# SSM phase tables built behind the first tables of the products, and an output stage in two equal parts of 516 tokens

## The chip, the cores and the metric

The kernel runs on one core of one Trainium2 chip. The metric is the device time of the whole program in microseconds (us), the median of several runs. PE is TensorE, DVE VectorE, ACT ScalarE, POOL GpSimd, SP the engine on which the DMAs are issued.

## The reference

One inference step of one decoder layer, for a prompt of 2048 tokens and 8 sample tokens of one position each, with D = 1024:

```python
h = rmsnorm(x, g_pre)
c_a, c_b, c_z, s_x, s_z, g_c, g_s = split(h @ w_in)   # 3 x 1024, 2 x 512, 2 x 1024 columns
u = c_a * sigmoid(c_b)
v = causal_depthwise_conv(u, 31 taps) + conv_b
y_c = (silu(layernorm(v)) * silu(c_z)) @ w_pc
ys = gelu(ssm(s_x))                    # 32 groups of 16 channels, 64 complex states each
ys = ys * sigmoid(ys @ w_glu + b_glu) * silu(s_z)
m = sigmoid(g_c) * y_c + sigmoid(g_s) * (ys @ w_ps)
x = x + rmsnorm(m @ w_out, g_post)
x = x + rmsnorm(p @ w_ple, g_ple) * sigmoid(x @ w_pg + b_pg)
```

The SSM is a diagonal complex recurrence. Its parameters are discretised first: exponentials, sine and cosine of `a * exp(log_dt)`, and from these the powers of each pole and its phase at 128 steps. Besides `y`, the last 30 inputs of the convolution and the last SSM states are returned.

## The kernel before

**Halves and products.** The tokens are taken in two halves: h=0 has 1024 prompt tokens and the 8 sample tokens, 1032 columns in three blocks of 344; h=1 has 1024, in two blocks of 512 (`BLOCKS`, line 213). Every large product is made in three passes, high x high, high x low, low x high (lines 288 to 290), accumulated in a PSUM bank. A weight tile of 128 x 1024 is loaded by DMA, its high part cast by ACT (`whi`, line 251), its low part subtracted on POOL (`wlo`, line 331 by way of `w_split`). `order` (lines 217 to 233) fixes the succession of weight tiles, which is that of the products: `w_ple`, the SSM's input SX, pairs CB and CA of the convolution's input, GC, SZ, `w_glu`, two GS tiles with a `w_ps` tile four times, CZ, `w_pc`, then `w_out` and `w_pg`, each as often as the output stage has parts.

**The planner.** All instructions are put out while the program is built, in an order that a planner finds (`Background`, lines 28 to 105). Products are the foreground. Everything else is written as generators that yield the engine they want next and the time at which their inputs are ready. The planner keeps a PE clock and one clock each for DVE (V), ACT (S) and POOL (G); `use(engine, cost)` books a step on its clock, with costs that are written into the code. After each block of products, `pump` puts out every background step whose start is not later than the PE clock, the smallest priority number first. Each engine then executes its instructions in that order. `cV(n)` is 0.08 + n/960, the booked cost of a DVE operation on n columns. `Units` is a pool of 38 buffers; `room(k)` waits in the plan until k are free.

**The SSM's tables.** `ssm_setup` (line 449) discretises the parameters, then builds the phase tables: a prelude (pole magnitudes `rho`, eight-step phases), and for each half x of the channels 7 doubling steps of `ph` (lines 566 to 588), stored by DMA in `ph_d`. After that it makes, for each batch b = 0 to 3 of 8 groups, the tables of the SSM's products: `gt` on DVE (line 601), transposed on PE (line 609), small products (line 619), `kd`, and on POOL `cq` (lines 646 to 651); each is stored by DMA. `ssm_batch` (line 675) loads them (`we`, `phu`), runs the products of a batch on PE (line 719), turns the result by the phases, scans, turns it back and runs the output products (lines 774 and 777).

**The convolution.** `conv_task` (line 820) has priority 10: for each of 8 channel tiles one operation at line 844 and taps at line 851, each an operation of DVE on 1024 columns, booked at 1.33. Where 8 or more units are free when a tile starts (line 839), `conv_side` (line 867) takes taps from the far end on ACT (lines 872 and 881) and POOL, and DVE adds the two sums; this is called the POOL partner below. The DVE operations between taps are evacuations of products: `u` (CA times the sigmoid of CB) and `gs` (`w_ps` times GS).

**Layer norm and `w_pc`.** `ln_task` (line 1262) follows the last convolution tile: sum, mean by a product, differences, squares, norm, and per tile the SiLU, the product with `cz`, and the split in `vh` and `vl`. `bg.drain(ln)` (line 1321) stands ahead of the `w_pc` products.

**The output stage** (lines 1378 to 1486). `parts` are runs of blocks. For every part all 8 tiles of `w_out` are run; `o_task` sums squares; `x1_task` and its tiles `x1_tile` (line 1395) norm, scale, add x and split into `mh` and `ml`. Then for every part the 8 tiles of `w_pg` are run over `x1`, and `y_task` (line 1442) makes `y`. `next_h_task` prepares h of the second half meanwhile. In the first half part 0 is one block of 344, part 1 two blocks of 344.

Of the kernel before, what the change touches and what calls it, by code (L numbers as in the profile page):

```python
# [27 lines left out]
class Background:  # L28
# [66 lines left out]
    def use(self, e, cost, ready=0.0):  # L95

        if e == "P":
            self.pe += cost
            self.now = max(self.now, self.pe)
            return self.pe + 0.25  # L100
        self.clock[e] = max(self.clock[e], ready) + cost
        return self.clock[e] + 0.2
# [31 lines left out]
def build(nc, tc, A, O):  # L134
# [23 lines left out]
    with ExitStack() as ctx:  # L158
# [17 lines left out]
        def tt(out, a, b, op=ALU.mult):  # L176
            V.tensor_tensor(out=out, in0=a, in1=b, op=op)  # L177

        def ts(out, a, s1, s2=None, op0=ALU.mult, op1=ALU.add):
            V.tensor_scalar(out=out, in0=a, scalar1=s1, scalar2=s2, op0=op0, **({} if s2 is None else {"op1": op1}))  # L180
# [32 lines left out]
        BLOCKS = [[(0, 344), (344, 344), (688, 344)], [(0, 512), (512, 512)]]  # L213
        PARTS = [[[0], [1, 2]], [[0], [1]]]
        TOK = [HT + NS, HT]

# [229 lines left out]

        tables = {"done": 0}

        def ssm_setup():
# [19 lines left out]
            exp_dve(mag, th, (k1, k2), ki)  # L469
            r0 = use("V", 5.6, 3.0)  # L470
            yield "V", r0
# [6 lines left out]
            ts(th, th, -3.1415925, 3.1415925, ALU.max, ALU.min)  # L478
            r0 = use("V", 1.6, r0)
            yield "S", r0  # L480
# [23 lines left out]
            tt(fim, k1, k3)  # L504
            r0 = use("V", 4.0, r0)
            yield "V", r0
# [17 lines left out]
            cmul(b3(bb, 0), b3(bb, 1), fb[0], fb[1], b3(bcu, 0), b3(bcu, 1), b3(bb, 2), b3(bb, 3))  # L524
            r0 = use("V", 6.0, r0)
            use("G", 1.5, r0)
# [13 lines left out]
            for b in range(NB):  # L540
                dma(out=tt_d[b], in_=zero.rearrange("p (q x) -> p q x", q=1).to_broadcast([P, 8, P]))

            yield "V", r0
            tt(k1, mag, mag)
            tt(k1, k1, k1)
            tt(rho, k1, k1)
            ph = [[k1, k2], [k3, nre]]

            def unit_length(re, im, t):

                tt(t[0], re, re)
                tt(t[1], im, im)
                tt(t[0], t[0], t[1], ALU.add)
                ts(t[0], t[0], -0.5, 1.5)
                tt(re, re, t[0])
                tt(im, im, t[0])

            v2 = [wk[:, x * 16:x * 16 + 16] for x in range(2)]
            V.tensor_copy(out=ph[0][0], in_=cs)
            V.tensor_copy(out=ph[0][1], in_=sn)  # L560
            for x in range(3):
                unit_length(*ph[0], v2)
                cmul(*ph[1], *ph[0], *ph[0], *v2)
                ph.reverse()
            r0 = use("V", 6.5, r0)
            for x in range(2):
                yield from room(3)
                pu2 = [alloc(name="ph") for _ in range(3)]
                un = [t[:, 0:1024].rearrange("p (j k) -> p j k", k=P) for t in pu2[0:2]]
                w2 = [pu2[2][:, y * 512:(y + 1) * 512].rearrange("p (j k) -> p j k", j=8) for y in range(2)]  # L570
                s2 = [t[:, 0:8] for t in v2]
                yield "V", r0
                for r in range(2):
                    V.tensor_copy(out=un[r][:, :, 0], in_=ph[0][r][:, x * 8:x * 8 + 8])
                m = 1
                while m < P:
                    unit_length(un[0][:, :, m - 1], un[1][:, :, m - 1], s2)
                    base = [u_[:, :, m - 1:m].to_broadcast([P, 8, m]) for u_ in un]
                    cmul(un[0][:, :, m:2 * m], un[1][:, :, m:2 * m], un[0][:, :, 0:m], un[1][:, :, 0:m],
                         *base, w2[0][:, :, 0:m], w2[1][:, :, 0:m])  # L580
                    m *= 2
                    r0 = use("V", 2.0 + 6 * cV(4 * m), r0)
                    yield "V", r0
                for b in range(2 * x, 2 * x + 2):
                    for r in range(2):
                        dma(out=ph_d[b][:, r * 512:(r + 1) * 512],
                            in_=pu2[r][:, (b - 2 * x) * 512:(b - 2 * x + 1) * 512], after=r0)
                free(*pu2)
            r1 = max(r0, r1)
            for b in range(NB):  # L590
# [65 lines left out]
                tables["done"] = b + 1  # L656
                tables[b] = queue["data"] + 1.0
            free(bb, bcu, cbd, pu)

# [15 lines left out]
        def ssm_batch(h, b, sx, ysb, n, ready):  # L675
# [24 lines left out]
            r = max(r, dma(out=we[:, 0:1024], in_=we_d[b], after=tables[b]))  # L700
            phu = alloc(name="sph")
            rp = dma(out=phu[:, 0:1024], in_=ph_d[b], after=tables[b])
            sc = alloc(name="sc")
# [24 lines left out]
            free(we)  # L728
            r = max(r1, rp)
            tmp, tm2 = alloc(name="stmp"), alloc(name="stmq")  # L730
# [348 lines left out]
        def half(h, hT, finish):  # L1079
# [300 lines left out]
            x1T = mT  # L1380
            parts = [[blocks[i] for i in p] for p in PARTS[h]]
            x1t = []
# [203 lines left out]
```

## Time and profile before

| what | value |
|---|---|
| time before, median of 3 runs | 1974.46 us (1973.43 to 1976.75) |
| the profiled execution's own time | 1971.99 us |
| its span in the profile | 1970.2 us |
| PE busy, share of the span | 97% |
| DVE busy, share of the span | 73% |
| granted PE clock over the span | 0.989 |

The profile shows one execution. PE is the engine that does the products, PEld its weight loads. A wait is the idle time of an engine before an instruction, put down to what ended it. The granted clock is a share of full speed: 1.00 is 2.4 GHz, 0.50 is 1.2 GHz. "L288" is line 288 of the kernel before.

### The profile page before, as it was taken

What the parts mean: (1) busy time and instruction counts of PE and PEld (TensorE: products, weight loads), DVE (VectorE), ACT (ScalarE), POOL (GpSimd) and SP (SyncE); (2) the same over time, 40 slices, a digit from 0 to 9 for tenths busy, and PEclk for the clock granted to TensorE, in tenths of its full rate; (3) what the DMA queues carried; (4) which work ended last, traced back from release to release, by engine and by line L of the source; (5) the groups of instructions that cost most, each with busy time, mean ns of one, the idle gap of its engine ahead of it and who ended that gap; (6) DMA issues with size and microseconds to landing.
All of it is one profiled execution on the core that took longest, in us unless ns stands there. A gap on an engine that the chain in (4) does not pass through costs nothing.

```text
span 1970.2 us, 26641 instructions
## 1 busy us (share of the span) xinstructions
PE 1918.5 (97%) x10386; PEld 1723.0 (87%) x10386; DVE 1442.1 (73%) x1696; ACT 765.6 (39%) x1276; POOL 784.8 (40%) x573
## 2 busy tenths in 40 slices
PE   8897999999999999999899999999999999999998
PEld 7797999999999999999798788888888888888877
DVE  6889997899899876444884479888589843442686
ACT  7424211227311364254532223444731353223542
POOL 1437623315422223253533222687743222224554
PEclk9998999999999999999899999999999999999999
DMA  8461344542122215342554463212212211422455
GB/s 315 155 203 62 100 133 141 177 144 78 51 83 78 102 50 193 116 142 93 190 197 164 172 200 123 74 60 91 71 48 75 97 67 43 160 107 77 148 189 174
DMA packets 103286, 243.58 MB, mean 124 GB/s; under 512 B 11752, under 2 KB 44648, under 8 KB 103144
## 3 DMA queue, kind: packets, MB, share of 16 engines
q1 hardware_dynamic: 102840, 241.68, 36.2%
q8 instruction: 81, 1.33, 0.3%
q14 instruction: 45, 0.37, 0.1%
q10 hardware_dynamic: 320, 0.20, 0.0%
HBM read 188.17 MB, written 54.62 MB: 123 GB/s over the span
## 4 chain that ended last, share of the span: by engine, by line
PE 85%; issue 4%; DVE 4%; POOL 2%; ACT 1%; DMA 1%; POOLq 0%; ACTq 0%; SPq 0%; DVEq 0%
PE bank L288 27%; PE bank L290 26%; PE bank L289 26%; PE bank L774 2%; POOL wlo L331 1%; PE bank L777 1%; PE bank L719 1%; DMA raw<-in_w 1%; POOL ca L331 1%; DVE sgp L331 1%; DVE o L183 0%; DVE o L331 0%; DVE ml L331 0%; DVE spar L183 0%; PE bank L308 0%
## 5 line engine op out<-in xcount | busy, mean ns | idle before, releaser
L331 POOL TENSOR_TENSOR wlo<-raw,whi 128x512 fp32r<-128x512 f32 x386 | 566.5, 1486 | 1082.2 <-ACT whi L251 1064.5
L288 PE MATMUL bank<-hh,whi 128*128 128x344 f32 (+1 forms) x1888 | 665.9, 353 | 0.9 <-ACT whi L251 0.9
L289 PE MATMUL bank<-hl,whi 128*128 128x344 f32 (+1 forms) x1888 | 659.9, 350 | 6.8 <-DVE hl L331 6.8
L290 PE MATMUL bank<-hh,wlo 128*128 128x344 f32 (+1 forms) x1888 | 661.2, 350 | 1.4 <-POOL wlo L331 1.4
L183 DVE SCALAR_TENSOR_TENSOR acc<-u,prm,acc 128x1024 f32<-128x1024 f32 x412 | 530.5, 1288 | 11.2
L289 PEld LDWEIGHTS bank<-hl,whi 128*128 128x128 f32 x1888 | 356.9, 189 | 39.4 <-DVE hl L331 7.1
L288 PEld LDWEIGHTS bank<-hh,whi 128*128 128x128 f32 x1888 | 356.4, 189 | 36.9 <-ACT whi L251 1.5
L290 PEld LDWEIGHTS bank<-hh,wlo 128*128 128x128 f32 x1888 | 356.8, 189 | 35.6 <-POOL wlo L331 2.4
L251 ACT CAST whi<-raw 128x512 fp32r<-128x512 f32 x388 | 223.9, 619 | 148.5 <-PE bank L289 68.6
L288 PE MATMUL bank<-mh,whi 128*128 128x344 f32 (+1 forms) x640 | 227.4, 355 | 7.7 <-ACT whi L251 5.8
L290 PE MATMUL bank<-mh,wlo 128*128 128x344 f32 (+1 forms) x640 | 227.1, 355 | 5.2 <-POOL wlo L331 5.1
L289 PE MATMUL bank<-ml,whi 128*128 128x344 f32 (+1 forms) x640 | 226.6, 354 | 0.3 <-DVE ml L331 0.3
L331 POOL TENSOR_TENSOR ca<-ca,cq 128x512 f32<-128x512 f32 x104 | 132.2, 1300 | 39.5 <-ACT cq L881 36.1
L288 PEld LDWEIGHTS bank<-mh,whi 128*128 128x128 f32 x640 | 122.6, 192 | 20.8 <-ACT whi L251 7.1
L290 PEld LDWEIGHTS bank<-mh,wlo 128*128 128x128 f32 x640 | 122.7, 192 | 18.9 <-POOL wlo L331 7.8
L289 PEld LDWEIGHTS bank<-ml,whi 128*128 128x128 f32 x640 | 122.5, 191 | 12.3 <-DVE ml L331 1.1
L289 PE MATMUL bank<-vl,whi 128*128 128x344 f32 (+1 forms) x320 | 111.9, 350 | 0.7 <-DVE vl L331 0.7
L288 PE MATMUL bank<-vh,whi 128*128 128x344 f32 (+1 forms) x320 | 112.2, 351 | 0.0
L290 PE MATMUL bank<-vh,wlo 128*128 128x344 f32 (+1 forms) x320 | 112.0, 350 | 0.0
L881 ACT ACTIVATE cq<-u,prm 128x512 f32<-128x512 f32 x104 | 73.4, 722 | 55.0 <-POOL ca L331 45.9
L331 DVE TENSOR_TENSOR oacc<-oacc,sq 128x344 f32<-128x344 f32 (+1 forms) x35 | 30.6, 874 | 79.2 <-ACT sq L1388 78.7
L177 DVE TENSOR_TENSOR gcl<-bank,gcl 128x344 f32<-128x344 f32 (+1 forms) x40 | 23.5, 587 | 65.7 <-PE bank L290 65.7
(213 smaller groups left out, 2447.7 us busy)
## 6 DMA issues: line engine op xcount, KB each, us to landing
raw<-in_w SPq DMA_DIRECT2D x194, 512.0 KB
cq<-cq SPq DMA_DIRECT2D x12, 512.0 KB
e<-e SPq DMA_DIRECT2D x8, 516.0 KB
rt<-e SPq DMA_DIRECT2D x8, 516.0 KB
gc<-gc SPq DMA_DIRECT2D x8, 516.0 KB
m<-gs SPq DMA_DIRECT2D x8, 516.0 KB
gcl<-gc SPq DMA_DIRECT2D x8, 516.0 KB
m2l<-m SPq DMA_DIRECT2D x8, 516.0 KB
```

Of the source, the lines that this page charges most:

```text
L177: V.tensor_tensor(out=out, in0=a, in1=b, op=op)
L183: V.scalar_tensor_tensor(out=out, in0=a, scalar=s, in1=b, op0=op0, op1=op1)
L251: S.copy(out=hi, in_=t[:, c])
L288: T.matmul(o, hi[:, w], rh[:, c0:c0 + n], start=kt == 0, stop=False)
L289: T.matmul(o, hi[:, w], rl[:, c0:c0 + n], start=False, stop=False)
L290: T.matmul(o, lo[:, w], rh[:, c0:c0 + n], start=False, stop=kt == k - 1)
L331: (V if e == "V" else GP).tensor_tensor(out=out, in0=a, in1=b, op=op)
L719: T.matmul(pvs[rr][half_[i], jj], we[:, g * P + rr * 64:g * P + rr * 64 + 64], U[:, g, 8:8 + ne], start=True, stop=True)
L774: T.matmul(pvs[i][:, jj], TW[:, :, 2 * j + i], U[:, 2 * j + i, o0:136], start=True, stop=False)
L777: T.matmul(pvs[i][:, jj], cq[half_[i], x * 512 + j * P:x * 512 + (j + 1) * P], X[half_[i], x, j, o0:136], start=False, stop=x == 1)
L881: S.activation(out=q[:, h], in_=u[:, k + x * 512:k + x * 512 + 512], func=AF.Identity, scale=w(k))
```

## The change

The prelude and the phase tables move. `phases(x)` becomes a function; the prelude and `phases(0)` stand behind the tables of b=0, `phases(1)` behind those of b=2. `ssm_batch` loads its phase tile after its first products instead of before them, and waits in the plan for `tables["phases"]`. The costs booked for the setup's and the phases' DVE work are raised. And the output stage of the first half gets its own blocks: two parts of 516 tokens, each of two blocks of 258, where it had parts of 344 and 688 in blocks of 344. The second half's stay as they were.

```diff
--- before.py
+++ after.py
@@ -212,6 +212,7 @@
         P_OF = {k: 8 // v for k, v in KT_OF.items()}
         BLOCKS = [[(0, 344), (344, 344), (688, 344)], [(0, 512), (512, 512)]]
         PARTS = [[[0], [1, 2]], [[0], [1]]]
+        OUT_PARTS = [[[(0, 258), (258, 258)], [(516, 258), (774, 258)]], [[(0, 512)], [(512, 512)]]]
         TOK = [HT + NS, HT]
 
         order = []
@@ -444,7 +445,7 @@
             ts(ki, k, 127.0, 8388608.0, ALU.add, ALU.mult)
             tt(out, q, ki.bitcast(F32))
 
-        tables = {"done": 0}
+        tables = {"done": 0, "phases": 0}
 
         def ssm_setup():
             yield from room(4)
@@ -467,7 +468,7 @@
             exp_dve(dt, k3, (k1, k2), ki)
             tt(th, are, dt)
             exp_dve(mag, th, (k1, k2), ki)
-            r0 = use("V", 5.6, 3.0)
+            r0 = use("V", 11.0, 3.0)
             yield "V", r0
             tt(th, aim, dt)
             ts(k1, th, 0.15915494309189535, MAGIC)
@@ -476,7 +477,7 @@
             stt(th, k1, -1.9350051879882812e-3, th, ALU.mult, ALU.add)
             stt(th, k1, -3.0199157663446332e-7, th, ALU.mult, ALU.add)
             ts(th, th, -3.1415925, 3.1415925, ALU.max, ALU.min)
-            r0 = use("V", 1.6, r0)
+            r0 = use("V", 2.5, r0)
             yield "S", r0
             S.activation(out=sn, in_=th, func=AF.Sin)
             S.activation(out=k1, in_=th, func=AF.Sin, scale=0.5)
@@ -502,7 +503,7 @@
             tt(k2, nre, aim)
             tt(k1, k1, k2, ALU.subtract)
             tt(fim, k1, k3)
-            r0 = use("V", 4.0, r0)
+            r0 = use("V", 7.0, r0)
             yield "V", r0
 
             def powers(t, top):
@@ -522,7 +523,7 @@
                     GP.tensor_copy(out=pwrev[r][:, p, :], in_=pw[r][:, 7 - p, :])
             fb = [f.rearrange("p (j x) -> p j x", x=1).to_broadcast([P, NJ, 16]) for f in (fre, fim)]
             cmul(b3(bb, 0), b3(bb, 1), fb[0], fb[1], b3(bcu, 0), b3(bcu, 1), b3(bb, 2), b3(bb, 3))
-            r0 = use("V", 6.0, r0)
+            r0 = use("V", 8.0, r0)
             use("G", 1.5, r0)
             GP.memset(zero, 0.0)
             yield from room(2)
@@ -539,31 +540,7 @@
             yield None, r1
             for b in range(NB):
                 dma(out=tt_d[b], in_=zero.rearrange("p (q x) -> p q x", q=1).to_broadcast([P, 8, P]))
-
-            yield "V", r0
-            tt(k1, mag, mag)
-            tt(k1, k1, k1)
-            tt(rho, k1, k1)
-            ph = [[k1, k2], [k3, nre]]
-
-            def unit_length(re, im, t):
-
-                tt(t[0], re, re)
-                tt(t[1], im, im)
-                tt(t[0], t[0], t[1], ALU.add)
-                ts(t[0], t[0], -0.5, 1.5)
-                tt(re, re, t[0])
-                tt(im, im, t[0])
-
-            v2 = [wk[:, x * 16:x * 16 + 16] for x in range(2)]
-            V.tensor_copy(out=ph[0][0], in_=cs)
-            V.tensor_copy(out=ph[0][1], in_=sn)
-            for x in range(3):
-                unit_length(*ph[0], v2)
-                cmul(*ph[1], *ph[0], *ph[0], *v2)
-                ph.reverse()
-            r0 = use("V", 6.5, r0)
-            for x in range(2):
+            def phases(x, r0):
                 yield from room(3)
                 pu2 = [alloc(name="ph") for _ in range(3)]
                 un = [t[:, 0:1024].rearrange("p (j k) -> p j k", k=P) for t in pu2[0:2]]
@@ -579,13 +556,17 @@
                     cmul(un[0][:, :, m:2 * m], un[1][:, :, m:2 * m], un[0][:, :, 0:m], un[1][:, :, 0:m],
                          *base, w2[0][:, :, 0:m], w2[1][:, :, 0:m])
                     m *= 2
-                    r0 = use("V", 2.0 + 6 * cV(4 * m), r0)
+                    r0 = use("V", 4.0 + 6 * m / 120.0, r0)
                     yield "V", r0
                 for b in range(2 * x, 2 * x + 2):
                     for r in range(2):
                         dma(out=ph_d[b][:, r * 512:(r + 1) * 512],
                             in_=pu2[r][:, (b - 2 * x) * 512:(b - 2 * x + 1) * 512], after=r0)
                 free(*pu2)
+                tables["phases"] = 2 * x + 2
+                tables["ph", x] = queue["data"] + 1.0
+                return r0
+
             r1 = max(r0, r1)
             for b in range(NB):
                 js = slice(b * 4, b * 4 + 4)
@@ -655,6 +636,33 @@
                 free(cq, wt)
                 tables["done"] = b + 1
                 tables[b] = queue["data"] + 1.0
+                if b == 0:
+
+                    yield "V", r0
+                    tt(k1, mag, mag)
+                    tt(k1, k1, k1)
+                    tt(rho, k1, k1)
+                    ph = [[k1, k2], [k3, nre]]
+
+                    def unit_length(re, im, t):
+
+                        tt(t[0], re, re)
+                        tt(t[1], im, im)
+                        tt(t[0], t[0], t[1], ALU.add)
+                        ts(t[0], t[0], -0.5, 1.5)
+                        tt(re, re, t[0])
+                        tt(im, im, t[0])
+
+                    v2 = [wk[:, x * 16:x * 16 + 16] for x in range(2)]
+                    V.tensor_copy(out=ph[0][0], in_=cs)
+                    V.tensor_copy(out=ph[0][1], in_=sn)
+                    for x in range(3):
+                        unit_length(*ph[0], v2)
+                        cmul(*ph[1], *ph[0], *ph[0], *v2)
+                        ph.reverse()
+                    r0 = use("V", 13.0, r0)
+                if b % 2 == 0:
+                    r0 = yield from phases(b // 2, r0)
             free(bb, bcu, cbd, pu)
 
 
@@ -698,8 +706,6 @@
             yield from room(4)
             we = alloc(name="swe")
             r = max(r, dma(out=we[:, 0:1024], in_=we_d[b], after=tables[b]))
-            phu = alloc(name="sph")
-            rp = dma(out=phu[:, 0:1024], in_=ph_d[b], after=tables[b])
             sc = alloc(name="sc")
             X = sc[:, 0:1096].rearrange("p (r j s) -> p r j s", r=2, j=4)
             yield "V", 0.0
@@ -726,7 +732,11 @@
                         S.copy(out=smp[:, rr, b * 4 + j0:b * 4 + j0 + 2, :], in_=pvs[rr][:, :, 128:136])
                     r1 = use("S", 0.56 if first else 0.36, r1)
             free(we)
-            r = max(r1, rp)
+            while tables["phases"] < b + 1:
+                yield None, bg.now + 1.0
+            yield from room(3)
+            phu = alloc(name="sph")
+            r = max(r1, dma(out=phu[:, 0:1024], in_=ph_d[b], after=tables["ph", b // 2]))
             tmp, tm2 = alloc(name="stmp"), alloc(name="stmq")
             E = X[:, :, :, 9:137]
             t1 = tmp[:, 0:1024].rearrange("p (r j s) -> p r j s", r=2, j=4)
@@ -1378,7 +1388,7 @@
             oT = [unit("o") for _ in range(NT)]
             acc = unit("oacc")
             x1T = mT
-            parts = [[blocks[i] for i in p] for p in PARTS[h]]
+            parts = OUT_PARTS[h]
             x1t = []
 
             def o_task(c, c0, m, r, sq):
```

## Rows read from the trace of the kernel before

**Rows 1.** The page's head and its table of engines: busy us, share, instructions.
```profile
span 1970.2 us, 26641 instructions
PE 1918.5 (97%) x10386; PEld 1723.0 (87%) x10386; DVE 1442.1 (73%) x1696; ACT 765.6 (39%) x1276; POOL 784.8 (40%) x573
```

**Rows 2.** Waits of PE over the span: us in total, times, longest.
```profile
PE bank L609 <- issue: 14.1, 1, 14.1
PE bank L288 <- ACT whi L251: 13.1, 6, 6.3
```

**Rows 3.** Windows: us, busy PE, PEld, DVE, ACT, POOL (instructions), PEclk, DMA, GB/s.
```profile
192.00:196.00 4.00, 0.00 (x0) 0.00 (x0) 3.82 (x9) 0.00 (x0) 0.00 (x0) 0.50 0.67 231
196.00:200.00 4.00, 3.83 (x15) 3.86 (x16) 3.93 (x7) 1.21 (x2) 1.28 (x1) 0.50 0.40 135
200.00:204.00 4.00, 4.00 (x23) 3.98 (x22) 3.93 (x5) 0.79 (x2) 0.00 (x0) 0.77 0.00 0
```

**Rows 4.** Windows of the first half's output stage, end of `w_out` and start of `w_pg`.
```profile
938.50:956.00 17.50, 17.35 (x108) 16.65 (x107) 10.06 (x8) 12.65 (x20) 11.70 (x8) 1.00 0.60 211
956.00:990.00 34.00, 23.32 (x103) 20.64 (x103) 33.03 (x34) 12.50 (x21) 17.15 (x10) 0.75 0.59 198
```

**Rows 5.** Windows in undisturbed products, columns of 344 and of 512.
```profile
650.00:700.00 50.00, 50.00 (x318) 50.00 (x318) 41.19 (x35) 22.48 (x34) 13.76 (x9) 1.00 0.27 96
1300.00:1350.00 50.00, 50.00 (x217) 40.47 (x216) 43.61 (x40) 24.39 (x38) 35.43 (x29) 1.00 0.21 74
```

**Rows 6.** Timeline of DVE, 105 to 195 us: start, us, operation, [idle before].
```profile
105.22 0.71 DVE L177 TENSOR_TENSOR spar<-spar 128x16 f32<-128x16 f32 x2
...
147.04 1.28 DVE L180 TENSOR_SCALAR acc<-u,prm 128x1024 f32<-128x1024 f32 x1
...
192.17 0.69 DVE L177 TENSOR_TENSOR ph<-ph 128x512 f32<-128x512 f32 x1
...
194.06 1.29 DVE L177 TENSOR_TENSOR gw<-pwr,bb 128x512 f32<-128x512 f32 x2
```

**Rows 7.** Timeline of DVE: the first half's last convolution and its end.
```profile
612.65 1.34 DVE L180 TENSOR_SCALAR acc<-u,prm 128x1024 f32<-128x1024 f32 x1
...
659.09 0.52 DVE L177 TENSOR_TENSOR gs<-bank,gs 128x344 f32<-128x344 f32 x1 [0.19 <-PE bank L290]
659.52 6.58 DVE L183 SCALAR_TENSOR_TENSOR acc<-u,prm,acc 128x1024 f32<-128x1024 f32 x5
666.14 1.28 DVE L183 SCALAR_TENSOR_TENSOR u<-u,prm,acc 128x1024 f32<-128x1024 f32 x1
```

**Rows 8.** Line 872 on ACT, 100 to 700 us: durations, first and last start.
```profile
L872 ACT ACTIVATE ca<-u,prm x1: 1234/1234/1234, 150.4 to 150.4; 128x1024 f32<-128x1024 f32 x1
```

**Rows 9.** Timeline of DVE: first operations of two successive convolutions, second half.
```profile
1342.69 1.28 DVE L180 TENSOR_SCALAR acc<-u,prm 128x1024 f32<-128x1024 f32 x1
...
1376.12 1.28 DVE L180 TENSOR_SCALAR acc<-u,prm 128x1024 f32<-128x1024 f32 x1
```

**Rows 10.** Timeline of PE and of DVE where `w_pc` begins.
```profile
751.59 0.32 PE L288 MATMUL bank<-vh,whi 128*128 128x344 f32 x1
...
755.93 0.43 PE L289 MATMUL bank<-vl,whi 128*128 128x344 f32 x1 [0.71 <-DVE vl L331]
...
752.28 1.23 DVE L331 TENSOR_TENSOR cz<-cz,u 128x1032 f32<-128x1032 f32 x1 [2.41 <-ACT cz L322]
```

**Rows 11.** Window from the last convolution operation to the last `vl`.
```profile
667.40:756.00 88.60, 87.89 (x558) 87.60 (x556) 65.61 (x49) 54.32 (x77) 26.83 (x15) 1.00 0.20 68
```

**Rows 12.** Chain of work that ended last: the small products of b=0.
```profile
207.40 1.70 PE bank L619 x16
```

**Rows 13.** Lines of DVE by form, 945.8 to 988.5 us: busy, mean ns.
```profile
L183 DVE SCALAR_TENSOR_TENSOR o<-o,prm,oacc 128x688 f32<-128x688 f32 x8 | 10.4, 1324 | 0.0
L331 DVE TENSOR_TENSOR o<-o,xr 128x688 f32<-128x688 f32 x8 | 10.0, 1275 | 0.0
L331 DVE TENSOR_TENSOR ml<-o,mh 128x688 fp32r<-128x688 f32 x8 | 8.9, 1138 | 0.8 <-ACT mh L338 0.8
```

## The prediction

> **What bounds the kernel now.** Four views, in this order. The engine table: PE is busy 1918.5 of 1970.2 us, DVE 1442.1 [rows 1]. So the kernel is a stream of matmuls, and a gain can only come from time in which that stream stands or runs slowly. The waits of PE over the whole span: one wait of 14.1 us at line 609, and 13.1 us in six waits for the ACT cast of a weight tile (line 251) [rows 2]. The windows around the first: PE has no matmul from 192 to 196 us, the granted clock is 0.50 there and in the next 4 us (1.2 of 2.4 GHz), and only 15 and 23 matmuls follow up to 204 us [rows 3]. The windows at the change from `w_out` to `w_pg` in the first half: 34.0 us from 956 hold 103 matmuls, at clock 0.75 [rows 4]; an undisturbed window, with columns of 344, holds 318 in 50 us, one every 0.1572 us, and with 512 columns 217, one every 0.2304 us [rows 5]. The change is aimed at these two places; the rest of PE's stream it leaves as it is.
>
> **Part 1: the stall at line 609.** PE waits there for `gt` of b=0, which DVE makes late: the phase prelude starts at 105.22, the last operation of the phases at 192.17, and `gt` only from 194.06 [rows 6]. After the change `gt` of b=0 stands directly behind the setup (about 105), and PE meets the transposes long after it. The 14.1 us go. At the slow clock, 38 matmuls ran from about 196.2 to 204, where 7.8/0.1572 = 50 would have: another 12 x 0.157 = 1.9 us. Together -16.0 us, and PE is that much earlier from there on.
>
> **Where that stall goes.** DVE does no less work; the prelude and the first half of the phases, which ran ahead of the first convolution operation (147.04 [rows 6]), now run behind or among it. In the code the convolution is filler (priority 10): a tap is emitted when the planner's V clock stands behind its PE clock, and evacuations are emitted between taps in the same in-order queue. Every microsecond booked for something else therefore moves a tap to a later place of PE's stream, whether or not DVE has time to spare. Bookings behind the first tap: after, two phase halves at 7 x 4.0 + 0.05 x 254 = 40.7, so 81.4; before, the last five steps of the second half (5 x 2.48 + 0.025 x 248 = 18.6), `gt` (3.7) and `kd` (0.8), which now lie ahead. Difference 58.3. (The prelude, 13, I place ahead of the first tap; behind it the figure is 71.) Two things give some back: the longer first convolution leaves its POOL partner about five more taps (6.7), and I allow 6 for gaps that nothing was booked in. So S = 45 us of taps, bounds 35 and 71.
>
> Before, the last evacuation of the `w_ps` products starts at 659.09, and six taps are behind it, to 667.4 [rows 7]. After, PE and that evacuation are 16.0 us earlier: 643.1. Behind it 8.3 us as before and the displaced taps, which run 1.28 us each [rows 7] where 1.33 is booked: 45 x 1.28/1.33 = 43.3. Against that, the last convolution now starts after those products have given units back, so it meets the condition of at least 8 free units and gets its POOL partner. Line 872, which opens a partner's work, runs once in the whole first half, for the first convolution [rows 8]; in the second half a convolution with partner takes 1376.12 - 1342.69 = 33.4 us [rows 9], where the last of the first half takes 667.4 - 612.65 = 54.8 without [rows 7]. Without the evacuations among them I put this at 31 against 48: -17. Convolution end: 643.1 + 8.3 + 43.3 - 17 = 677.7, against 667.4.
>
> Then the layer norm, which is serial. Before, it runs from 667.4 to the last `vl` at 755.9, 88.5 us. Out of this come 2.4 us in which DVE waited for the last `cz` [rows 10] and 3.5 for two sums of the next half's norm, which I guess fall elsewhere; 82.6 remain. Lower bound 65.6, DVE's busy time there [rows 11]; upper 88.5. PE wants that last `vl` 3.5 us after its first `w_pc` matmul (it started at 751.59 and then waited 0.71 us for it [rows 10]). So `w_pc` can start at 677.7 + 82.6 - 3.5 = 756.8. PE stands ready at 751.6 - 16.0 = 735.6: a new wait of about 21 us, behind which the slow clock costs 1.9 us again, as in [rows 3]. Compared with 751.6 + 0.7 = 752.3 before, that is +4.5 + 1.9 = **+6.4 us for the move and the bookings together**, the 16.0 us spent within it. The bounds: S alone moves it by -10 to +25, the layer norm by -17 to +6, a missing partner by +17; it cannot go below -16.7, no wait at all.
>
> The other edits of this part: `ssm_batch` takes its phase tile after its first products and waits for the table there, the same two DMAs on SP's queue, later; only this batch's own products are behind that wait. The raised bookings of the setup (+11.3) change no instruction and lie ahead of the first tap. Both cost nothing as long as the tables of b=3 are there before PE comes to its products; the price if not is case E.
>
> **Part 2: columns of 258.** Per product 8 tiles x 24 x 3 blocks become x 4; with two products 1152 matmuls become 1536, for the same columns. The line through the two prices of [rows 5] has 0.000436 us per column, so 258 costs 0.1572 - 86 x 0.000436 = 0.1197 us. 1536 x 0.1197 = 183.9 against 1152 x 0.1572 = 181.1: **+2.8 us**. No row shows 258. The bound below is the nearest row of matmuls with few columns, each with a weight load of its own, 16 in 1.70 us [rows 12]: 0.106, so -18 us; the bound above is no gain from fewer columns, 0.157: +60. I take the line, since both its rows are products of the same kind.
>
> The Trainium skill ("TensorE: Matmul & The Clock Gate", Back-to-back issue gap) says that in a stream with weight loads the formula N/2.4 + 2.5 ns under-counts at small N, 81 ns instead of 56 at 128 columns. Adding those 25 ns at 258 gives an estimate of 135 ns, and +26 us in place of +2.8; the rows of 344 and 512 lie only 11 and 15 ns above the formula, so the trace does not bear that addition out. It is the mechanism of case D.
>
> **What the equal parts give.** Before, part 0 of `w_pg` has 8 x 24 x 0.1572 = 30.2 us of products to cover what DVE and then ACT do for `x1` of part 1: 24 operations over 688 tokens, 29.3 us [rows 13], with `y` tiles of part 0 between them, DVE busy 33.0 of 34.0 us [rows 4]. Weight casts wait in ACT's in-order queue behind the `mh` casts that wait for DVE. From 938.5 to 990 PE did 211 matmuls in 51.5 us [rows 4]: 51.5 - 211 x 0.1572 = 18.3 us lost. After: part 0 covers 8 x 48 x 0.1197 = 46.0 us; the stretch of that DVE work, 42.7 us before [rows 13], is 42.7 x 516/688 = 32, and with one more `y` tile about 36, starting some 7 us in: ready at 43 of 46. The order of the queue on ACT remains, so I keep 6 us of loss (2 to 14): **-12.3 us**. Weight tiles are asked for at a slower pace in the first part (5.7 us each, not 3.8) and a faster one in the second (not 7.5); I cost that at nothing, hidden by the cast that runs a tile ahead, and if it is not, it is part of the 14.
>
> **Sum.** +6.4 + 2.8 - 12.3 = -3.1 us. On the profiled execution's own time, 1971.99 (its span and 1.8 around it), that is 1968.9; this execution lies 2.5 below the median of the runs, so **1971**. 0.2% is 3.9 us, about what a measurement of this kernel can tell from no change.
>
> **The cases** (on the median's scale).
> A, the sum above: the stall moves to `w_pc`, the output stage gains. Chance 0.45; its own range 1960 to 1982.
> B, no new wait, because the displaced taps reach the layer norm in time after all: -16.7 + 2.8 - 12.3 = -26, 1948. For it: DVE is busy 41.2 of 50 us from 650 [rows 5], so it has some time in hand. Against: an in-order queue uses that time only if taps stand there. 0.20.
> C, the other side: the last convolution finds fewer than 8 free units and gets no partner. The convolution then ends 17 us later, at 695, the wait at `w_pc` is 38 us and the sum -3 + 17 = +14: 1988. It decides as soon as the partner saves less than 10 of those 17. For it: in the first half seven of eight have none [rows 8]. 0.18.
> D, columns of 258 do not follow the line: at 0.140 us the sum is -3 - 2.8 + 33.9 = +28, 2002, more at 0.157. 0.07.
> E, PE meets a table that is not ready: those of b=3 now stand behind the second half of the phases, and batch 3's products block all that is behind them in PE's queue. A stall as at line 609, about 15 us: 1986. 0.10.
>
> Faster by over 0.2%: nearly half of A and all of B, 0.42. Within it: 0.3 of A, 0.15. Slower: the rest of A, with C, D and E, 0.43. The range 1949 to 1994 leaves out part of B, D, and a tail of C.
>
> **What would show it.** In the new profile: no wait at line 609 and clock 1.00 at 196 us; 20 to 35 taps behind the last `gs` evacuation; a second run of line 872 in the first half, around 640 to 670 us; a wait ahead of the first `w_pc` matmul that begins near 735 and ends near 757; 258 columns every 0.12 us; some 6 us of loss, not 18, where `w_out` gives over to `w_pg`. Wrong would be: no wait at `w_pc` (B) or near 40 us (C), a wait for tables of a later batch (E), a pace of 0.13 or more (D).

## The result and the profile after

The changed kernel takes 2010.35 us (median of 4 runs, 2009.56 to 2010.9) against 1973.95; the ratio is 1.0181, 95% interval 1.0164 to 1.0199. The forecast was 1971.0, a little faster, with a range of 1949 to 1994: the kernel became slower, and the time lies above the range. The profiled execution took 2010.22 us at a granted clock of 0.982; its span and its engines:

```profile
span 2008.0 us, 27539 instructions
PE 1931.1 (96%) x10772; PEld 1728.9 (86%) x10772; DVE 1428.2 (71%) x1676; ACT 814.0 (41%) x1362; POOL 855.5 (43%) x627
```

The 384 additional matmuls are there ([rows 1] has 10386). Where the time went is read from the first matmul of each stage in the two timelines of PE:

| stretch | before | after | difference |
|---|---|---|---|
| start to the first product on `hh` | 56.7 | 58.7 | +1.9 |
| SX to SZ of the first half, with the SSM | 443.1 | 442.5 | -0.7 |
| `w_glu` to the end of CZ | 251.9 | 250.9 | -1.0 |
| `w_pc`, with the wait ahead of it | 92.0 | 127.4 | **+35.4** |
| `w_out` and `w_pg`, first half | 204.6 | 191.4 | **-13.2** |
| SX to SZ of the second half | 398.3 | 412.9 | **+14.6** |
| the rest | 523.5 | 524.3 | +0.7 |

The waits of PE over the span (us in total, times, longest; line numbers up to 449 are one higher than before, later ones about ten):

```profile
PE bank L289 <- ACT vh L339: 23.2, 3, 14.6
PE bank L289 <- ACT whi L252: 8.2, 3, 6.8
PE bank L289 <- DVE u L177: 8.1, 2, 5.4
PE bank L787 <- DVE sc L177: 7.0, 3, 4.4
...
PE bank L290 <- DVE vl L332: 5.1, 3, 2.8
...
PE bank L784 <- DMA tw<-tt: 1.9, 1, 1.9
```

The 14.1 us at line 609 of [rows 2] are gone. In their place stand waits that the kernel before did not have, or hardly (0.7 us for `vl`): for `u`, a product that finds no free bank because DVE has not evacuated one; for `vh` and `vl`, the layer norm ahead of `w_pc`; for `sc`, the SSM of the second half. The windows at the first and at the largest (columns as in [rows 3]) show the clock falling with them:

```profile
170.00:180.00 10.00, 4.57 (x33) 4.09 (x32) 9.11 (x47) 2.48 (x7) 2.76 (x3) 0.82 0.00 0
180.00:190.00 10.00, 10.00 (x64) 9.60 (x63) 3.59 (x18) 3.50 (x9) 4.55 (x4) 0.84 0.10 20
755.00:800.00 45.00, 18.71 (x71) 14.95 (x72) 34.62 (x33) 23.86 (x25) 3.85 (x3) 0.58 0.23 80
```

DVE around the first of these waits (timeline):

```profile
107.05 3.48 DVE L177 TENSOR_TENSOR gw<-pwr,bb 128x512 f32<-128x512 f32 x2
...
114.57 0.69 DVE L177 TENSOR_TENSOR gt<-gw 128x512 f32<-128x512 f32 x1
131.11 0.52 DVE L177 TENSOR_TENSOR u<-bank,sg 128x344 f32<-128x344 f32 x1 [15.85 <-PE bank L291]
...
162.42 1.53 DVE L177 TENSOR_TENSOR spar<-spar 128x16 f32<-128x16 f32 x2
...
176.29 1.27 DVE L177 TENSOR_TENSOR spar<-spar 128x16 f32<-128x16 f32 x8
177.47 0.93 DVE L177 TENSOR_TENSOR u<-bank,sg 128x344 f32<-128x344 f32 x2
```

`gt` of b=0 is there at 115, 80 us sooner than in [rows 6]. But then DVE stands idle for 15.9 us, where the kernel before ran steps of the phases; the prelude now runs from 162.4 to 177.5, and two evacuations stand behind it. PE waited until 178.0.

And DVE at the end of the convolution:

```profile
660.30 0.52 DVE L177 TENSOR_TENSOR gs<-bank,gs 128x344 f32<-128x344 f32 x1 [0.17 <-PE bank L291]
660.73 13.21 DVE L183 SCALAR_TENSOR_TENSOR acc<-u,prm,acc 128x1024 f32<-128x1024 f32 x10
...
677.50 1.27 DVE L180 TENSOR_SCALAR acc<-u,prm 128x1024 f32<-128x1024 f32 x1
...
684.98 27.78 DVE L183 SCALAR_TENSOR_TENSOR acc<-u,prm,acc 128x1024 f32<-128x1024 f32 x21
712.86 1.23 DVE L177 TENSOR_TENSOR u<-acc,ca 128x1024 f32<-128x1024 f32 x1
...
789.55 1.23 DVE L332 TENSOR_TENSOR vl<-cz,vh 128x1032 fp32r<-128x1032 f32 x1 [1.12 <-ACT vh L339]
```

Six taps stood behind the last `gs` evacuation in [rows 7]; here 32 do, and the convolution ends at 714.0 although its last tile got a partner.

### The profile page after: what moved, and what is told of

Its sections match the earlier page's. It is cut to its first block, busy times and chain, and to the rows that moved or that the text cites. A ratio compares the mean times of both kernels' runs of the same rounds, so it can differ in the third digit from the quotient of the medians.

```text
span 2008.0 us, 27539 instructions
## 1 busy us (share of the span) xinstructions
PE 1931.1 (96%) x10772; PEld 1728.9 (86%) x10772; DVE 1428.2 (71%) x1676; ACT 814.0 (41%) x1362; POOL 855.5 (43%) x627
## 4 chain that ended last, share of the span: by engine, by line
PE 73%; DVE 14%; issue 4%; POOL 2%; DMA 2%; ACT 1%; SPq 0%; POOLq 0%; ACTq 0%; DVEq 0%
PE bank L289 23%; PE bank L290 23%; PE bank L291 23%; DVE acc L183 2%; POOL wlo L332 2%; PE bank L784 1%; DVE ph L177 1%; DVE sc L760 1%; PE bank L787 1%; DVE sc L177 1%; DVE spar L177 1%; DMA raw<-in_w 1%; DVE sgp L332 1%; DVE stmq L177 1%; DVE stmp L177 1%
## 5 line engine op out<-in xcount | busy, mean ns | idle before, releaser
L183 DVE SCALAR_TENSOR_TENSOR acc<-u,prm,acc 128x1024 f32<-128x1024 f32 x385 | 495.6, 1287 | 10.3
L291 PEld LDWEIGHTS bank<-hh,wlo 128*128 128x128 f32 x1888 | 357.7, 189 | 36.3 <-POOL wlo L332 2.5
L289 PE MATMUL bank<-mh,whi 128*128 128x258 f32 (+1 forms) x768 | 246.6, 321 | 2.2 <-ACT mh L339 1.7
L291 PE MATMUL bank<-mh,wlo 128*128 128x258 f32 (+1 forms) x768 | 246.5, 321 | 1.7 <-POOL wlo L332 1.6
L290 PE MATMUL bank<-ml,whi 128*128 128x258 f32 (+1 forms) x768 | 246.3, 321 | 0.4 <-DVE ml L332 0.3
L332 POOL TENSOR_TENSOR ca<-ca,cq 128x512 f32<-128x512 f32 x158 | 209.5, 1354 | 58.0 <-ACT cq L891 55.6
L289 PEld LDWEIGHTS bank<-mh,whi 128*128 128x128 f32 x768 | 145.6, 190 | 14.1 <-ACT mh L339 1.9
L290 PEld LDWEIGHTS bank<-ml,whi 128*128 128x128 f32 x768 | 145.6, 190 | 12.5 <-DVE ml L332 1.2
L891 ACT ACTIVATE cq<-u,prm 128x512 f32<-128x512 f32 x158 | 111.9, 722 | 81.2 <-POOL ca L332 77.6
L289 PEld LDWEIGHTS bank<-vh,whi 128*128 128x128 f32 x320 | 61.7, 193 | 30.1 <-ACT vh L339 24.3
L332 DVE TENSOR_TENSOR oacc<-oacc,sq 128x258 f32<-128x258 f32 (+1 forms) x42 | 29.7, 723 | 69.6 <-ACT sq L1398 69.3
```

The source lines that it names most:

```text
L183: V.scalar_tensor_tensor(out=out, in0=a, scalar=s, in1=b, op0=op0, op1=op1)
L289: T.matmul(o, hi[:, w], rh[:, c0:c0 + n], start=kt == 0, stop=False)
L290: T.matmul(o, hi[:, w], rl[:, c0:c0 + n], start=False, stop=False)
L291: T.matmul(o, lo[:, w], rh[:, c0:c0 + n], start=False, stop=kt == k - 1)
L332: (V if e == "V" else GP).tensor_tensor(out=out, in0=a, in1=b, op=op)
L891: S.activation(out=q[:, h], in_=u[:, k + x * 512:k + x * 512 + 512], func=AF.Identity, scale=w(k))
```

## The experiments

Each ran beside the kernel before on the same chip; ratios are to that. "Loss at `w_pc`" is the wait ahead of its first matmul plus what its 576 matmuls took over 92 us; SX to SZ are the stretches of the table above. Three theories were to be told apart: the equal parts cost the second half its 14.6 us; the new order costs; the bookings cost.

**1. The parts alone** (kernel before).

```diff
-            parts = [[blocks[i] for i in p] for p in PARTS[h]]
+            parts = OUT_PARTS[h]
```

> The kernel before with the two equal parts of 258-column blocks alone. Theory 1 (all of the loss comes from the tables' new place and the raised bookings): the output stage falls from 204.8 us by the 13.2 us seen in the changed kernel, nothing else moves, about 1961 us. Rival 2 (the 14.6 us that the second half's first products lost come from what the new parts leave over for it): the gain is given back there, 1974 us or more.

1961.04 us, ratio 0.9942 (0.9927 to 0.9957). The output stage falls to 192.1 us, SX to SZ of the second half stay at 398.6. The equal parts are a clean gain and have no part in the loss.

**2. The tables' part alone** (changed kernel, the diff above reversed).

> The changed kernel with the output stage's old parts. Theory 1: it loses the 13.2 us again, about 2023 us, w_pc still waits some 35 us, and the second half still loses about 14 us. Rival 2: the second half is as before, about 2009 us.

2021.12 us, ratio 1.0246 (1.0231 to 1.0261). Loss at `w_pc` 36 us, second half 409.4. As theory 1 had it.

**3. The bookings alone** (kernel before, the six raised values; one of them is shown).

```diff
-                    r0 = use("V", 2.0 + 6 * cV(4 * m), r0)
+                    r0 = use("V", 4.0 + 6 * m / 120.0, r0)
```

> The kernel before with the raised bookings alone (no instruction is changed, only the order in which the planner puts them out). If every booked microsecond behind the first tap moves a tap: five steps raised by 7.6 + 6.2 = 13.8 us, so the layer norm ends about 14 us later against a slack of 2, the wait at line 609 stays or grows, 1983 to 1990 us. Rival (the order alone does it): within 4 us of before.

2054.01 us, ratio 1.0411 (1.0395 to 1.0427), far more than either had said, and at another place. SX to SZ of the first half take 518 us; the waits:

```profile
PE bank L777 <- DVE sc L177: 39.5, 2, 38.6
PE bank L719 <- DMA swe<-we: 16.4, 1, 16.4
```

`gt` of b=3 is made at 442.5 us, 99 later than in the kernel before, and PE waits for that batch's table; its scans then stand behind 28 operations of two convolutions in DVE's queue (460 to 499 us), and PE waits for `sc`. SZ and all else lie behind these products. That is case E, from the bookings and without the new order. `w_pc` loses 10 us.

**4. The order alone** (kernel of run 2 with the six old bookings; one is shown).

```diff
-                    r0 = use("V", 4.0 + 6 * m / 120.0, r0)
+                    r0 = use("V", 2.0 + 6 * cV(4 * m), r0)
```

> The tables in their new place with the old bookings, old output parts. If the bookings move the taps: 41 of the 58 us by which the plan moved remain out, the wait at w_pc falls from 35 to about 10 us, 1985 to 1998 us. Rival (the order alone does it): as with the raised bookings, about 2020 us.

2011.04 us, ratio 1.0189 (1.0172 to 1.0206). Loss at `w_pc` is only 12 us, as forecast, though the time is not in the band; PE waits 10.2 us for `u` and 8.5 for `gt` earlier, and the first half's SX to SZ take 459. With low bookings DVE is late in front, with high ones late at the end. In both, the second half takes 409 to 411 us.

**5. The phase tile early, in the second half** (changed kernel; only added lines are shown).

```diff
+            if not first:
+                phu = alloc(name="sph")
+                rp = dma(out=phu[:, 0:1024], in_=ph_d[b], after=tables[b])
             sc = alloc(name="sc")
...
+            if first:
+                while tables["phases"] < b + 1:
+                    yield None, bg.now + 1.0
+                yield from room(3)
+                phu = alloc(name="sph")
+                rp = dma(out=phu[:, 0:1024], in_=ph_d[b], after=tables["ph", b // 2])
+            r = max(r1, rp)
```

> The changed kernel, but in the second half ssm_batch takes its phase tile before its first products again (the tables have long been there). Theory A (the late tile leaves more units free, the convolution's POOL partner starts earlier, beside the SSM's scans, which slow from 3.1 to 10 us): the second half's first products fall from 413 us to 398 to 400, the whole to about 1996 us. Rival B (the later w_pc or something else in the order does it): they stay at 411 to 413, the whole at 2010.

1997.33 us, ratio 1.0123 (1.0108 to 1.0138): 13 us back. SX to SZ of the second half take 400.5. Line 882 is the start of a partner (line 872 before); in the second half, of the changed kernel and then of this run (887 there):

```profile
L882 ACT ACTIVATE ca<-u,prm x7: 1235/1240/1263, 1178.9 to 1433.7; 128x1024 f32<-128x1024 f32 x7
```

```profile
L887 ACT ACTIVATE ca<-u,prm x5: 1235/1245/1257, 1251.8 to 1398.6; 128x1024 f32<-128x1024 f32 x5
```

Two partners more, the first 70 us sooner, among the SSM's batches. The same scans, eight each, in the changed kernel beside POOL and without it (POOL busy 10.00 of 10 us from 1250, 0.00 from 1283), on DVE's timeline:

```profile
1247.80 10.07 DVE L760 TENSOR_TENSOR_SCAN sc<-rho,sfin,sc 128x128 f32<-128x128 f32 x8
...
1283.56 3.10 DVE L760 TENSOR_TENSOR_SCAN sc<-rho,sfin,sc 128x128 f32<-128x128 f32 x8
```

The first scan above took 0.47 us, each of the other seven went with one operation of POOL, 1.37 us apart. All scans of the second half (busy us, mean ns of one), in the changed kernel and in this run:

```profile
L760 DVE TENSOR_TENSOR_SCAN sc<-rho,sfin,sc 128x128 f32<-128x128 f32 x32 | 22.5, 770 | 0.0
```

```profile
L765 DVE TENSOR_TENSOR_SCAN sc<-rho,sfin,sc 128x128 f32<-128x128 f32 x32 | 12.4, 461 | 0.0
```

In the kernel before they take 12.4 us too. PE's waits for `sc` in the second half, 7.0 us in the changed kernel, are gone. Theory A holds.

**6. Only the second half of the phases behind b=0's tables** (kernel of run 1, old bookings; two waits for free units added).

```diff
+            r0 = yield from phases(0, r0)
...
+                if b == 0:
+                    r0 = yield from phases(1, r0)
                 tables["done"] = b + 1
```

> The kernel before with the equal parts, and only the second half of the phases moved behind the tables of b=0, old bookings. If the stall at line 609 was time that DVE has to give back (theory 1: this stretch is bound by DVE, and bookings below the true cost only move the stall): the 14 us wait goes, other waits of 8 to 18 us for DVE come, 1955 to 1966 us. Rival (the stall is a mere matter of order): 16 us less than with the equal parts alone, 1945 us.

1975.05 us, ratio 1.0014 (1.0005 to 1.0023), 14 us slower than run 1 and above both expectations. The wait at 609 shrinks to 7.4 us in three pieces, and `u` (4.5) and `whi` (7.6) are new. Moving the stall wins nothing.

**7. No partner for the first convolution** (kernel of run 1; one wait for a free unit added).

```diff
-                if units.left() >= 8:
+                if units.left() >= 8 and (h or c):
```

> The kernel before with the equal parts, and no POOL partner for the first convolution. If the second half of the phases takes 50 us, not 27, because POOL works beside it: the phases run at the quiet price, gt is there 15 to 20 us sooner, the wait at line 609 goes; but about 13 taps more on DVE, of which w_pc sees up to 15 us: 1950 to 1962 us. If POOL has no part in it: the phases take 45 to 50 us as before, the wait stays, and 1961 to 1976 us.

1970.17 us, ratio 0.9987 (0.9978 to 0.9997). The last operation of the phases:

```profile
171.07 0.69 DVE L177 TENSOR_TENSOR ph<-ph 128x512 f32<-128x512 f32 x1
```

It starts 21 us sooner than in [rows 6]. The phases' 172 operations add up to 51.4 us here and to 74.5 in the kernel before. No wait is left at line 609, and SX to SZ end 16 us earlier than in run 1: what the forecast had promised of the change. `w_pc` then loses 25, since DVE has the partner's taps too, and so the time falls into the rival's band, though the phases rule the rival out.

**8. Taps booked less** (changed kernel).

```diff
-                    r = use("V", 1.33)
+                    r = use("V", 1.33 if h else 1.2)
```

> The changed kernel, with the first half's taps booked at 1.20 in place of 1.33 (no instruction changed). If the wait at w_pc is made by the place of the taps in DVE's queue and not by a lack of DVE time: some 200 taps x 0.13 = 26 us of plan come back, the 35 us lost at w_pc fall to about 10, 1985 us. If DVE's time is the bound: new waits for evacuations take its place, 2005 us or more.

2076.07 us, ratio 1.0523 (1.0507 to 1.0538). Loss at `w_pc` 12 us, as the first theory said, but the SSM's products wait in front, 36.3 us for a table's DMA and 26.0 for `sc` the longest. The place of the taps sets the wait at `w_pc`, but the taps cannot come earlier at no cost: they stand ahead of the last batch's tables (`gt` of b=3 at 434 us, 357 in the changed kernel) and of its scans. That DVE lacked the time is not shown; from 300 to 400 us it is busy for 63 us of the 100, 79 in the changed kernel.

**9. The first partner waits for the phases** (kernel of run 1; the flag is set behind both halves).

```diff
+            while "phases" not in tables:
+                yield None, bg.now + 0.5
             yield "S", r
```

> The kernel before with the equal parts; the first convolution keeps its POOL partner, but the partner starts only once the phase tables are put out, so that POOL does not work for it beside the phases. If sharing with POOL is what made the phases long: they take 30 us or less per half, the wait at line 609 goes as without a partner (PE 16 us earlier), the partner still takes some 5 to 8 taps, and w_pc gives back less than the 25 us of that run: about 1953 us (1948 to 1960). Rival (POOL's work only meets other DVE operations later, so nothing is won): 1958 to 1966 us.

1957.32 us, ratio 0.9918 (0.9905 to 0.9932). The time lies at the edge of both bands; the phases decide. They add up to 51.5 us, the partner starts at 173.7 us, 151.3 in run 1, and of the stall is left:

```profile
PE bank L611 <- DVE gt L177: 2.4, 1, 2.4
```

SX to SZ end 8.5 us earlier than in run 1, not 16, and `w_pc` loses 8. Sharing with the partner made the stall; that this is POOL's work, and not ACT's, is read from the rows of the last section.

**10. A partner for the seventh convolution** (changed kernel).

```diff
-                if units.left() >= 8:
+                if units.left() >= (3 if not h and c == 6 else 8):
```

> The changed kernel; the seventh of the first half's eight convolutions also gets a POOL partner, with 3 free units in place of 8. If the wait at w_pc is set by the number of taps left on DVE behind the last evacuation: a partner takes some 13 taps, 17 us, the 35 us lost at w_pc fall to about 18, the whole to 1993 us. Rival (POOL's work slows what runs beside it, or the plan only moves other work there): 2003 us or more.

1995.97 us, ratio 1.0115 (1.0101 to 1.0129). Loss at `w_pc` 22 us, 13 less; the partner took ten taps off DVE, where 13 were expected and 17 us.

**11. and 12. Late partners on run 9** (3 free units are enough from the fifth convolution on; for the seventh alone; two waits for free units added).

> As the run whose first partner waits for the phases, and from the fifth convolution of the first half on 3 free units are enough for a partner (the fifth and the seventh get one). If DVE's work is the bound up to w_pc: two partners take some 20 taps, the wait at w_pc goes, 1945 to 1950 us. Rival (units are taken from others, or POOL slows DVE): as without them or slower, 1953 to 1962 us.

> As the run whose first partner waits for the phases, with one more partner in the first half, for the seventh convolution only (3 free units are enough there). The run with two more lost nothing at w_pc, but about 6 us elsewhere. If the earlier of those two partners cost it: 1950 to 1954 us, with no loss at w_pc. If the later one alone already takes units or slows DVE: 1956 to 1960 us.

1957.19 us, ratio 0.9917 (0.9903 to 0.993), and 1951.31 us, ratio 0.989 (0.9873 to 0.9906). Both lose nothing at `w_pc`; the first loses as much elsewhere. Run 12 beats both kernels; where its longest waits stand:

```profile
PE bank L289 <- ACT whi L252: 8.3, 3, 6.9
PE bank L290 <- DVE hl L332: 6.7, 1, 6.7
PE bank L291 <- POOL wlo L332: 3.0, 5, 1.1
PE bank L778 <- DVE u L177: 2.3, 1, 2.3
```

**13. The changed kernel without its first partner** (edit of run 7).

> The changed kernel without a POOL partner for the first convolution. If the prelude and phases, now beside the partner, are what makes DVE late for the u evacuation: the prelude takes about 9 us in place of 15, the waits of PE for u (5.4 and 2.6 us) go, and the first products end some 10 us sooner; the first convolution has about 13 taps more on DVE, so w_pc's loss stays or grows: 1998 to 2015 us. Rival (those waits come from the order of the queue alone): they stay, 2012 to 2025 us.

2028.84 us, ratio 1.0278 (1.0263 to 1.0294). Both waits for `u` are gone, the phases' operations add up to 44.8 us in place of 75.7, and SX to SZ of the first half end 4.9 us sooner, where 10 were expected: PE now waits 4.8 and 3.4 us for DMAs of tables. The loss at `w_pc` grows to 63 us, 28 more and beyond what was expected. DVE at the end of the last convolution, and PE's wait at the products of a mean:

```profile
701.43 37.06 DVE L183 SCALAR_TENSOR_TENSOR acc<-u,prm,acc 128x1024 f32<-128x1024 f32 x28
738.52 1.28 DVE L183 SCALAR_TENSOR_TENSOR u<-u,prm,acc 128x1024 f32<-128x1024 f32 x1
```

```profile
PE bank L364 <- ACT nh L339: 22.4, 2, 21.0
```

The late partner went to the seventh convolution (its first ACT operation at 655.4 us); the last has none and ends at 739.8, 25.8 later than in the changed kernel. That is the mechanism of case C. The wait of 21.0 us is the layer norm's second mean, at a time when PE has no other product left.

**14. The prelude ahead again** (changed kernel, the block from `tt(k1, mag, mag)` to `use("V", 13.0, r0)` moved up in front of the loop over b).

> The changed kernel with the prelude alone put back ahead of the tables of b=0, where DVE otherwise stands idle for 16 us. If taps are displaced by what is booked behind the first of them: 13 us less behind it, the wait for u at 178 us goes (5.4 and about 2 of slow clock), and w_pc loses some 12 us less, 1988 to 1996 us. Rival (w_pc's loss does not follow what is booked there): 2003 us or more.

2016.87 us, ratio 1.022 (1.0203 to 1.0237): a miss. The wait at 178 us goes, but PE waits 6.2 us for `gt` at 222, and 5.1 and 7.2 for `tw` and `sc` near 450. Loss at `w_pc` 32 us, only 3 less. Thirteen booked microseconds do not come back as thirteen.

## Why the prediction was wrong

**"PE is 16.0 us earlier from there on": failed.** The wait went, the gain did not come: SX to SZ were 0.7 us shorter. The step took the stall for a matter of order, `gt` behind the phases. What made it was the phases' price: 23 of their 74.5 us came from the convolution's partner beside them (runs 7 and 9). Moved, they cost 75.7 beside the same partner, and DVE, idle where they had stood, was late for `u` instead (run 13: without the partner those waits are gone). Without the partner 16 us come back in the old order (run 7), in the new one only 4.9, as other waits take their place (run 13): the price is shown as the cause of the old stall, and for a part only of what was lost after the move. Runs 4, 6 and 14 each bring a stall back somewhere else. The text had the rows for this, line 872 first at 150.4 us [rows 8] and the phases ending at 192, and did not put them together.

**"A new wait of about 21 us" at `w_pc`: right in kind, mis-sized, 35.4 with the clock against 23.** The last evacuation came at 660.3, not 643.1, by the step above. Behind it the work lasted to 714.0, 53.7 us where 34.6 were forecast: 32 taps in place of some 27, and sums and sample operations that were not counted. The partner came as forecast (line 882 starts at 679.5). The layer norm took 76.8 us to the last `vl`, less than the 82.6 forecast. So the convolution's end was 36.3 us too early in the forecast, the layer norm 5.8 too long, and PE, ready at 752.0, came 16.4 later than thought: 14 more in all. PE waited more than once: it started at 767.6 and stopped again inside `w_pc` for late tiles. The prelude, which the text placed ahead of the first tap, ran behind it (162.4 us, first tap 142.3); by the text's own sum S was then 13 larger. But run 14 put it ahead again and got 3 back: that every booked microsecond moves a tap by as much is shown for the direction (runs 3, 4, 8) and not for the amount.

**"Both cost nothing" for the late phase tile: failed, 14.6 us.** The step looked at queues and waits in the first half alone. The second half runs the same code; there the tile's later allocation left 8 units free sooner, partners started among the scans, which took 22.5 us in place of 12.4, and DVE was late for the SSM's products (run 5). All kernels with the new order and the late tile in both halves have 409 us or more there; all others have 397 to 402.

**The output stage: right.** +2.8 - 12.3 = -9.5 was forecast, -13.2 measured. The line for 258 columns held, 0.118 to 0.121 us a matmul:

```profile
930.00:945.00 15.00, 15.00 (x124) 14.89 (x124) 7.89 (x11) 8.51 (x20) 6.74 (x5) 1.00 0.42 130
985.00:1000.00 15.00, 15.00 (x127) 15.00 (x126) 14.93 (x16) 7.87 (x16) 8.04 (x6) 1.00 0.47 158
```

PE's waits for `whi` (5.3 us) and `wlo` (3.4) in this stage are gone; the one for `mh` stays, 1.7 us where it was 1.9. Case D, a pace of 0.13 or more, is refuted for this width.

**The sum.** Forecast -3.1, measured +38.2 on the two profiled executions. Between them lie 14 us from PE's lead that did not come, 13 from `w_pc`, 15 from the second half, -4 from the output stage; 3 lie at the start and the end (the start takes 56.7 to 59.4 us over all runs). Of the cases none was it: a loss near C's 38 us came at `w_pc`, but not for its reason.

What stays open: why run 3's bookings put the tables off so far, and what else in the new order holds SX to SZ up in run 13; neither was followed further. That the second half's partners slow the scans by POOL's work rests on the rows of run 5, not on a run that takes POOL's work alone away there.

## What to carry to other kernels

Before a stalled step is moved, ask what makes it long: here an engine that worked beside it. Keeping that engine away until the step was done, 22 us, removed most of the stall (run 9); moving the step only brought others. A planner's prices hold for one neighbourhood only; where work is moved beside another engine, take its price from rows with that engine busy. And an allocation that is moved in shared code changes who gets the free buffers in every later pass, so every pass is to be costed.

## What the runs showed of the hardware

Some operations of DVE take the pace of POOL's while POOL works. In the kernel before, two small operations on DVE's timeline, without the partner's adds on POOL and beside them:

```profile
145.35 0.17 DVE L177 TENSOR_TENSOR spar<-spar 128x8 f32<-128x8 f32 x1
148.71 0.17 DVE L180 TENSOR_SCALAR spar<-spar 128x8 f32<-128x8 f32 x1
...
153.76 1.15 DVE L177 TENSOR_TENSOR spar<-spar 128x8 f32<-128x8 f32 x1
154.94 1.21 DVE L180 TENSOR_SCALAR spar<-spar 128x8 f32<-128x8 f32 x1
```

The last two end at 154.91 and 156.16; POOL's adds, about 1.3 us each, end at 154.88 and 156.13. ACT's work for the partner has no such ends there (154.36 and 155.64). Eight scans took 10.07 us and 3.10; while the taps, whose second tensor lies in PSUM (`acc`), took 1.25 to 1.29 us in every run. The Trainium skill ("SBUF — State Buffer", Who interferes with whom) states that a VectorE instruction with two SBUF inputs contends with a GpSimd instruction that reads SBUF, that the ports they share are an exclusive lock, and that the order of issue decides who blocks. The trace agrees: the price of the short operations rises to about that of one POOL add, whatever their size, and the taps, with one tensor in SBUF, are not touched. But the TENSOR_SCALAR, which reads a single tensor, slowed as well; the sentence on two inputs does not cover it.
